# Banded attention: one sequence of projection pieces for all pairs, kept two pieces ahead of the tiles

## The chip, the cores and the metric

The kernel runs on one core of a Trainium2 chip. Its engines are TensorE (PE: matmuls, with their weight loads, PEld), VectorE (DVE), ScalarE (ACT), GpSimd (POOL) and SyncE (SP, which issues most DMAs). Each takes its instructions in order and waits for the others by semaphores. The metric is the time of one execution on the device in microseconds, less is better. Three runs of the kernel before took 1625.54 to 1629.71 us, 1628.01 in the median.

## The reference

One layer of a bidirectional encoder over 1024 tokens of width 1024, in float32. The part that the change touches, shortened:

```python
h = rms_norm(x)
q_lat, kv_lat, q_b, k_b, v_b, gate_a, gate_b = split(h @ w_in)
o_a = mla_branch(q_lat, kv_lat, ...)      # dense attention, 8 heads
# windowed branch: 16 heads of 64, 4 key/value heads, |i-j| <= 128
s = q @ k.T * scale + bias;  s = where(valid, s, -1e30)
p = softmax(concat([s, sink]))[..., :span]
o_b = p @ v
mixed = sigmoid(gate_a) * o_a + sigmoid(gate_b) * o_b
x = x + mixed @ w_out                     # then a convolutional FFN
```

## The kernel before

Float32 operands are split into a rounded high part and the rest (`split`: a cast on ScalarE, L132, and a subtraction on VectorE, L133), and a product is three matmuls on these parts. The kernel goes through norm and latents, the banded (windowed) branch with the projections of gates, queries and keys, the dense branch, and the FFN. The change is in the banded branch, from about 138 to 534 us of the span.

The banded branch goes over 8 pairs of heads (`t`, 0 to 7) and in each over 8 tiles of 128 rows (`n`, 0 to 7). A tile has three stages on TensorE. `s1` makes the scores of the next tile (L138, `sc`) and hands them to VectorE (L657: bias, mask and minimum), ScalarE (L661: two exponentials with their sums) and GpSimd (L666: normalisation). `s2` turns the tile's probabilities with five transposes into the one PSUM buffer `ptw` (L679) and splits them in three parts, one wide (128x512) and two narrow (64x128), into `pth` (L132) and `ptl` (L133). `s3` multiplies the previous tile's parts with the values (`po`); ScalarE copies half of that (L702), VectorE adds (L704), and half a pair at a time VectorE multiplies by a gate (L709).

Between the stages stand pieces of the projections `h @ w_in` for the gates of this pair and the queries of the next: a generator `project` makes one 128x512 block in 24 matmuls (L446), and it yields after every six, a piece. With a block's last piece comes its end: a copy on VectorE for a gate (L507) and later a sigmoid on ScalarE (L511), a cast (L493) and a subtraction (L494) per half for queries, and twice two of each for keys (L474 to L477). Weights come by DMA (L106), are cast on ScalarE (L110, `whi`) and subtracted on GpSimd (L113, `wlo`); the queue of buffers lets them run ahead. Exponential and sigmoid need different tables on ScalarE, so each sigmoid among the exponentials brings two table loads.

A pair has 24 pieces and 24 stages, and behind each stage one piece follows (L764 to L766). Pair 3 makes the keys for pairs 4 to 7 in place of two gate blocks; pair 7 makes those two, spreads 22 of its 24 pieces over the stages and hands the rest to the end, where buffers of the normed input are refilled for the dense branch.

The order on TensorE is the program's up to tile 5 of pair 7 (`manual_schedule`); on the other engines, and on TensorE after that, a scheduler orders the instructions as it thinks they become ready.

Of the kernel before, what the change touches and what calls it, by code (L numbers as in the profile page):

```python
# [23 lines left out]
NT = S // P  # L24
KD = D // P
# [20 lines left out]
C_GA = C_V + KV_B * HD_B  # L46
C_GB = C_GA + D
# [13 lines left out]
FIRST = "PE Activation".split()  # L61
ORDER = 'b0 a0 A0 d0 b1 a1 A1 d1'.split()
PRE = 2
END = 22
DEFER = 3
ABS = 2
# [8 lines left out]
def f32(ap):  # L75
    return ap.bitcast(F32)
# [3 lines left out]
def encoder_layer(ctx, tc, x, positions, norm1_g, w_in, q_a_norm_g, w_q_b, kv_a_norm_g, w_kv_b,  # L80
# [101 lines left out]
    def big(shape, name):  # L182
        return hp.tile(shape, F32R, tag="big", bufs=4, name=name)
# [233 lines left out]
    def absorbing(u):  # L417
        h = u % H_A
        return weights4(wqk_d.rearrange("k p h c -> p k h c")[:, :, h:h + 4, :], 2, 4, P)
# [4 lines left out]
    def absorb_into(u, pair, pj):  # L424
        qs[u] = pair
        h, hf = u % H_A, u // H_A
        tok = slice(hf * 512, (hf + 1) * 512)
        terms = []
        for k in range(2):
            wh, wlo = [w[:, k, h % 4] for w in wqk[u // 4]]  # L430
            terms += [(wh, lt["h"][:, k, tok]), (wh, lt["l"][:, k, tok]), (wlo, lt["h"][:, k, tok])]
        three(pj, terms)
        split(pair[0], pair[1], pj)


    with ExitStack() as pa:
# [3 lines left out]
        def project(w, hf, post):  # L440
            hi, lo = w()
            pj = ps.tile([P, 512], F32, tag="pj", bufs=3, name="pj")
            tok = slice(hf * 512, (hf + 1) * 512)
            for k in range(KD):
                for j, (a, b) in enumerate(((hi, ht_h[hf]), (hi, ht_l[hf]), (lo, ht_h[hf]))):
                    nc.tensor.matmul(pj, a[:, k, :], b[:, k], start=(k + j == 0), stop=(k == KD - 1 and j == 2))  # L446
                if k % 2 == 1:
                    if k == KD - 1:
                        post(pj, tok)
                    yield  # L450

        def once(c0):
            got = []

            def w():
                if not got:
                    got.append(columns(w_in, c0, P))
                return got[0]
            return w
# [3 lines left out]
        def keys(g):  # L463
            w = once(C_K + g * HD_B)

            def post(pj, tok):
                if tok.start == 0:
                    for gg in (g, g + 1):
                        kws[gg] = [ap_.tile([P, S], F32R, tag="kw", bufs=6, name="kw") for _ in range(2)]
                for j in range(2):  # L470
                    kh, kl = kws[g + j]
                    a = slice(j * HD_B, (j + 1) * HD_B)
                    b = slice((1 - j) * HD_B, (2 - j) * HD_B)
                    nc.scalar.copy(kh[a, tok], pj[a, :])  # L474
                    nc.scalar.copy(kh[b, tok], pj[a, :])
                    nc.vector.tensor_tensor(kl[a, tok], pj[a, :], f32(kh[a, tok]), op=ALU.subtract)
                    nc.vector.tensor_tensor(kl[b, tok], pj[a, :], f32(kh[a, tok]), op=ALU.subtract)  # L477
            return [project(w, hf, post) for hf in range(2)]
# [3 lines left out]
        def queries(t):  # L482
            w = once(C_Q + t * P)

            def post(pj, tok):
                hf = tok.start // 512
                qss[t, hf] = ap_.tile([P, 512 // HQ, 2, HQ], F32R, tag="qs", bufs=4, name="qs")
                for j in range(2):
                    q_ = qss[t, hf][:, :, j]
                    a = slice(j * HD_B, (j + 1) * HD_B)  # L490
                    b = slice((1 - j) * HD_B, (2 - j) * HD_B)
                    src = pj[a, :].rearrange("p (m c) -> p m c", c=HQ)
                    nc.scalar.mul(q_[a], src, HD_B ** -0.5)  # L493
                    nc.vector.scalar_tensor_tensor(q_[b], src, HD_B ** -0.5, f32(q_[a]),  # L494
                                                   op0=ALU.mult, op1=ALU.subtract)
            return [project(w, hf, post) for hf in range(2)]
# [3 lines left out]
        def gates(t, name, c0):  # L500
            w = once(c0 + t * P)

            def post(pj, tok):
                hf = tok.start // 512
                g_ = ap_.tile([P, 512], F32, tag="g", bufs=6, name="g")
                gts[t, name, hf] = g_
                nc.vector.tensor_copy(g_, pj)  # L507
                apart = t == DEFER
                if (name, hf) == ("a", 1) or (apart and hf == 1):
                    for nm_, h_ in ((name, 0), (name, 1)) if apart else (("b", 0), ("b", 1), ("a", 0), ("a", 1)):  # L510
                        nc.scalar.activation(gts[t, nm_, h_], gts[t, nm_, h_], AF.Sigmoid)  # L511
                    for h_ in range(2 if name == "a" else 0):
                        nc.sync.dma_start(ga_d[t][:, h_ * 512:(h_ + 1) * 512], gts.pop((t, "a", h_)))
            return [project(w, hf, post) for hf in range(2)]
# [89 lines left out]
        def dense_start(j):  # L604
            if j == 1:
                for j in range(2):
                    lt[j] = big([P, H_A, 512], f"qr{j}")
                    for c in range(0, H_A, 2):
                        nc.sync.dma_start(f32(lt[j][:, c:c + 2]), qr_d[j][:, c:c + 2])
                return  # L610
            for nm_, d_ in (("h", lt_d[0]), ("l", lt_d[1])):
                lt[nm_] = big([P, 4, S], "lt_" + nm_)
                for c in range(4):
                    nc.sync.dma_start(f32(lt[nm_][:, c]), d_[:, c])
            return
            yield

        def absorb_early(u):
            raw = wp.tile([P, 2, 512], F32R, tag="raw", bufs=2, name="qearly")
            absorb_into(u, [raw[:, j] for j in range(2)], ps.tile([P, 512], F32, tag="pj", bufs=3, name="pje"))  # L620
            return
            yield
# [89 lines left out]
        def drain(gen):  # L712
            for _ in gen:
                pass
# [16 lines left out]
        drain(q0_[0])  # L731
        s1(0, 0)
        drain(q0_[1])
        def steps():
            for t in range(KD):
                gb, ga = gates(t, "b", C_GB), gates(t, "a", C_GA)
                if t < KD - 1:
                    q_ = queries(t + 1)
                    gens = [gb[0], gb[1], ga[0], q_[0], ga[1], q_[1]]
                    if t == DEFER:  # L740
                        gens = [gb[0], gb[1], q_[0], q_[1]]
                    total = 24
                    if t % 4 == 3:
                        gens += keys((t + 1) // 2)
                        total = 24
                else:
                    gens = [dict(b=gb, a=ga, A=gates(DEFER, "a", C_GA), d=[dense_start(0), dense_start(1)])[c][int(i)] for c, i in ORDER] + [absorb_early(u) for u in range(PRE)]
                    total = END
                chain_ = (None for gen in gens for _ in gen)
                done, pos = 0, 0  # L750
                for n in range(NT):
                    for stage in range(3):
                        if stage == 0:
                            if n + 1 < NT:
                                s1(t, n + 1)
                            elif t + 1 < KD:
                                s1(t + 1, 0)
                        elif stage == 1:
                            s2(t, n)
                        elif n > 0:  # L760
                            s3(t, n - 1)
                        elif t > 0:
                            s3(t - 1, NT - 1)
                        pos += 1  # L764
                        while done < math.ceil(total * pos / 24):
                            next(chain_, None)  # L766
                            done += 1
                    if n == NT - 1:
                        drain(chain_)
                    if (t, n) == (KD - 1, ABS):  # L770
                        wqk[0] = absorbing(0)
                    yield t, n

        todo = steps()
        with tc.manual_schedule(engines={mybir.EngineType.PE}):
            while next(todo) != (KD - 1, MANUAL):
# [54 lines left out]
    with ExitStack() as pb:  # L831
# [143 lines left out]
        for i in range(ni):  # L975
            u, qt = i // 4, i % 4
# [30 lines left out]
        u = ni // 4 - 1  # L1007
# [151 lines left out]
    gens = [preps(f) for f in range(NF)]  # L1159
# [205 lines left out]
    with ExitStack() as pe_:  # L1365
# [40 lines left out]
        for gi, group in enumerate(groups):  # L1406
# [3 lines left out]
            for bank, phase, outs in phases:  # L1410
# [9 lines left out]
                for j, tp in turns_:  # L1420
                    if up_ and j == 0:
                        banks[bank, tp] = ps.tile([P, 512], F32, tag=bank, bufs=4, name="b" + bank)
                    a, w = opers[j]
# [5 lines left out]
                for tp in range(4):  # L1429
                    b_ = banks[bank, tp]  # L1430
                    i = outs[0] * 4 + tp
# [49 lines left out]
```

## Time and profile before

| | |
|---|---|
| runs | 1625.54, 1628.01, 1629.71 us |
| profiled execution | 1627.23 us, span 1625.5 us |
| busy, share of the span | PE 1583.6 us (97%), DVE 1121.9 (69%), ACT 902.8 (56%), POOL 539.8 (33%) |
| largest groups of the banded branch | projections (L446) x416 of each of three forms, 169.2, 164.4 and 164.0 us |

The times of a group are sums over its instructions. Matmuls are pipelined: one of 128x512 is shown with 0.39 to 0.40 us, and the next starts 0.23 us after it. An idle time in brackets is that of the engine just before the row's instruction, with what ended it. Engines wait for each other, so a busy share says little by itself; the waits of TensorE say where time can be won. The page's clock line shows TensorE at full clock in every slice.

### The profile page before, as it was taken

The numbers are of one execution on the slowest core, as the hardware profiler recorded it, in microseconds if no ns is written. First come the engines' busy times: TensorE is split into PE (matmuls) and PEld (weight loads), VectorE is DVE, ScalarE is ACT, GpSimd is POOL, SyncE is SP. The second block draws the span as 40 slices with busy tenths as digits, with TensorE's granted clock in tenths as the row PEclk, the third lists the DMA queues.
The fourth block names the chain that finished last, engine by engine and source line by source line (L and its number), as shares of the span: only waits on it lengthen the run. The fifth ranks groups of instructions, "written<-read, shape, count | busy, mean of one in ns | idle before, by whom it ended". The sixth has DMA issues, their size and how long they took to land.

```text
span 1625.5 us, 21901 instructions
## 1 busy us (share of the span) xinstructions
PE 1583.6 (97%) x7714; PEld 1306.1 (80%) x7714; DVE 1121.9 (69%) x2024; ACT 902.8 (56%) x1688; POOL 539.8 (33%) x487
## 2 busy tenths in 40 slices
PE   8999999999999899999999999999999999999998
PEld 7887888878888778888887777888888888778886
DVE  6575655666655576666663388777777777799997
ACT  6446777777777565555552255445444444443445
POOL 3113343434342475656562000344443343000011
PEclk9999999999999999999999999999999999999999
DMA  8472211111213551113124883222222221652402
GB/s 272 123 208 73 66 51 58 52 56 51 69 47 131 192 196 61 62 50 129 52 78 156 291 297 91 78 79 79 90 79 78 78 91 65 262 193 77 156 1 104
DMA packets 151893, 179.57 MB, mean 110 GB/s; under 512 B 10711, under 2 KB 112903, under 8 KB 151784
## 3 DMA queue, kind: packets, MB, share of 16 engines
q1 hardware_dynamic: 149160, 169.59, 31.8%
q0 software_dynamic: 2624, 8.59, 1.6%
q8 instruction: 61, 1.00, 0.3%
q14 instruction: 48, 0.39, 0.1%
HBM read 126.74 MB, written 51.41 MB: 110 GB/s over the span
## 4 chain that ended last, share of the span: by engine, by line
PE 68%; ACT 4%; DVE 4%; DMA 3%; issue 1%; SPq 0%; POOL 0%; ACTq 0%; DVEq 0%
PE bx L1155 15%; PE byz L1155 11%; PE sc L138 9%; PE bx L1427 6%; PE po L138 6%; PE by L1427 6%; PE pj L446 5%; PE pt L876 3%; PE py L138 2%; DMA mh<-mx_d 1%; PE pjq L138 1%; PE pyb L138 1%; PE ptw L679 1%; DMA x_d<-xt 1%; PE pjo L138 1%
## 5 line engine op out<-in xcount | busy, mean ns | idle before, releaser
L1155 PE MATMUL bx<-hs,op 128*128 128x512 f32 x1056 | 258.6, 395 | 0.9 <-ACT hs L1203 0.7
L1155 PEld LDWEIGHTS bx<-hs,op 128*128 128x128 f32 x1056 | 198.0, 188 | 49.6 <-ACT hs L1203 0.9
L1155 PE MATMUL byz<-hs,op 128*128 128x512 f32 x792 | 196.3, 395 | 0.0
L1155 PEld LDWEIGHTS byz<-hs,op 128*128 128x128 f32 x792 | 148.6, 188 | 36.4 <-DVE hs L788 0.4
L446 PE MATMUL pj<-ht_h,whi 128*128 128x512 f32 x416 | 169.2, 407 | 0.0
L446 PE MATMUL pj<-ht_h,wlo 128*128 128x512 f32 x416 | 164.4, 395 | 0.0
L446 PE MATMUL pj<-ht_l,whi 128*128 128x512 f32 x416 | 164.0, 394 | 0.0
L862 POOL TENSOR_TENSOR p<-p,rib 128x1024 f32<-128x1024 f32 x64 | 123.4, 1938 | 119.2 <-DVE rib L861 99.0
L788 POOL TENSOR_TENSOR op<-wu,op 128x512 fp32r<-128x512 f32 x38 | 48.9, 1298 | 273.4 <-DVE cg L791 149.4
L132 ACT CAST pT<-pt 128x512 fp32r<-128x512 f32 x128 | 73.5, 589 | 92.0 <-PE pt L876 91.9
L133 DVE TENSOR_TENSOR ptl<-ptw,pth 64x128 fp32r<-64x128 f32 (+2 forms) x176 | 74.4, 423 | 72.0 <-ACT pth L132 69.9
L788 POOL TENSOR_TENSOR op<-s,op 128x512 fp32r<-128x512 f32 x57 | 99.0, 1736 | 66.0 <-ACT op L1026 65.8
L133 DVE TENSOR_TENSOR pT<-pt,pT 128x512 fp32r<-128x512 f32 x128 | 86.8, 682 | 46.2 <-ACT pT L132 46.1
L1427 PE MATMUL bx<-op,op 128*128 128x512 f32 x480 | 113.6, 394 | 3.3 <-ACT cv L1350 1.8
L1427 PEld LDWEIGHTS bx<-op,op 128*128 128x128 f32 x480 | 90.9, 190 | 23.7 <-ACT cv L1350 2.2
L113 POOL TENSOR_TENSOR wlo<-raw,whi 128x512 fp32r<-128x512 f32 x66 | 85.4, 1321 | 65.6 <-ACT whi L110 65.2
L1427 PE MATMUL by<-op,op 128*128 128x512 f32 x444 | 103.6, 389 | 0.0
L854 DVE TENSOR_REDUCE nmb<-sc 128x1 f32<-128x1024 f32 x64 | 78.3, 1224 | 35.4 <-PE sc L138 34.9
L666 POOL TENSOR_TENSOR st<-st,ri 128x640 f32<-128x640 f32 x48 | 60.1, 1251 | 115.7 <-DVE ri L663 115.5
L1427 PEld LDWEIGHTS by<-op,op 128*128 128x128 f32 x444 | 83.1, 188 | 17.9 <-DVE x L791 0.4
L138 PE MATMUL po<-pT,ct 128*128 128x512 f32 x384 | 94.6, 395 | 0.0
L138 PE MATMUL sc<-lt_h,q 128*128 128x512 f32 x224 | 93.5, 417 | 1.2 <-ACT p L859 1.2
(297 smaller groups left out, 3651.2 us busy)
## 6 DMA issues: line engine op xcount, KB each, us to landing
wu<-in_w_up_dram SPq DMA_DIRECT2D x44, 512.0 KB, 3.8
raw<-in_w_in_dram SPq DMA_DIRECT2D x29, 512.0 KB, 3.9
act_d<-t SPq DMA_DIRECT2D x22, 512.0 KB, 2.6
ra<-act_d SPq DMA_DIRECT2D x22, 512.0 KB, 5.1
rw<-in_w_down_dram SPq DMA_DIRECT2D x22, 512.0 KB, 4.9
mh<-mx_d SPq DMA_DIRECT2D x16, 512.0 KB, 5.2
mh<-mx_d SPq DMA_DIRECT2D x12, 448.0 KB, 3.5
xt<-in_x_dram SPq DMA_DIRECT2D x8, 512.0 KB
```

What stands on the lines that cost most here:

```text
L113: nc.gpsimd.tensor_tensor(lo[:, q], raw[:, q], f32(hi[:, q]), op=ALU.subtract)
L132: nc.scalar.copy(hi, src)
L133: nc.vector.tensor_tensor(lo, src, f32(hi), op=ALU.subtract)
L138: nc.tensor.matmul(ps, a, b, start=(i == 0), stop=(i == n - 1))
L446: nc.tensor.matmul(pj, a[:, k, :], b[:, k], start=(k + j == 0), stop=(k == KD - 1 and j == 2))
L666: nc.gpsimd.tensor_tensor(pn, pn, ri[:, :, None].broadcast_to([P, 2, BAND]), op=ALU.mult)
L788: eng.tensor_tensor(dst, a, b, op=ALU.subtract)
L854: nc.vector.tensor_reduce(nm, sc, axis=AX.X, op=ALU.max, negate=True)
L862: nc.gpsimd.tensor_tensor(pe, pe, ri.broadcast_to([P, S]), op=ALU.mult)
L876: nc.tensor.transpose(pt[:, c, :], pe[:, kcol:kcol + P], ident)
L1155: nc.tensor.matmul(bank, a[:, i, k], hs[c][:, j, k], start=(start and k + n == 0), stop=(k == 3 and n == 2), skip_group_check=not start)
L1427: nc.tensor.matmul(banks[bank, tp], l_, r_, start=(up_ and j + n == 0), stop=(j == len(group) - 1 and n == 2), skip_group_check=not up_)
```

## The change

The pieces of all pairs form one sequence, made by the new function `pieces`, and each stage takes pieces up to its own place plus `LEAD_A`, which is 2. So three pieces stand behind the first stage, one behind each further stage, and the last pair ends its pieces two stages earlier. Before, each pair had its own sequence, which ended with the pair's last stage. What is computed is the same.

```diff
+LEAD_A = 2
...
@@ -731,23 +732,20 @@
         drain(q0_[0])
         s1(0, 0)
         drain(q0_[1])
+        def pieces(t):
+            gb, ga = gates(t, "b", C_GB), gates(t, "a", C_GA)
+            if t == KD - 1:
+                made = dict(b=gb, a=ga, A=gates(DEFER, "a", C_GA), d=[dense_start(0), dense_start(1)])
+                return [made[c][int(i)] for c, i in ORDER] + [absorb_early(u) for u in range(PRE)]
+            q_ = queries(t + 1)
+            if t == DEFER:
+                return [gb[0], gb[1], q_[0], q_[1]] + keys((t + 1) // 2)
+            return [gb[0], gb[1], ga[0], q_[0], ga[1], q_[1]]
+
         def steps():
+            chain_ = (None for t in range(KD) for gen in pieces(t) for _ in gen)
+            done = 0
             for t in range(KD):
-                gb, ga = gates(t, "b", C_GB), gates(t, "a", C_GA)
-                if t < KD - 1:
-                    q_ = queries(t + 1)
-                    gens = [gb[0], gb[1], ga[0], q_[0], ga[1], q_[1]]
-                    if t == DEFER:
-                        gens = [gb[0], gb[1], q_[0], q_[1]]
-                    total = 24
-                    if t % 4 == 3:
-                        gens += keys((t + 1) // 2)
-                        total = 24
-                else:
-                    gens = [dict(b=gb, a=ga, A=gates(DEFER, "a", C_GA), d=[dense_start(0), dense_start(1)])[c][int(i)] for c, i in ORDER] + [absorb_early(u) for u in range(PRE)]
-                    total = END
-                chain_ = (None for gen in gens for _ in gen)
-                done, pos = 0, 0
                 for n in range(NT):
                     for stage in range(3):
                         if stage == 0:
@@ -761,11 +759,12 @@
                             s3(t, n - 1)
                         elif t > 0:
                             s3(t - 1, NT - 1)
-                        pos += 1
-                        while done < math.ceil(total * pos / 24):
+                        pos = 3 * n + stage + 1
+                        due = (KD - 1) * 24 + math.ceil(END * pos / 24) if t == KD - 1 else t * 24 + pos
+                        while done < due + LEAD_A:
                             next(chain_, None)
                             done += 1
-                    if n == NT - 1:
+                    if (t, n) == (KD - 1, NT - 1):
                         drain(chain_)
                     if (t, n) == (KD - 1, ABS):
                         wqk[0] = absorbing(0)
```

The scheduled engines are ordered anew. The line numbers of the changed kernel are one higher there. On ScalarE, tile 1 of pair 1 before: from the wide cast of that tile's chain to that of the next. `pth` are the casts of the split, `kr` is the copy, `st` the exponentials, `g` the sigmoid, `whi` the cast of projection weights.

```order
L132 CAST pth<-ptw 128x512
L511 ACT_TABLE_LOAD
L511 ACTIVATE g<-g 128x512
L132 CAST pth<-ptw 64x128
L702 COPY kr<-po 64x256
L132 CAST pth<-ptw 64x128
L661 ACT_TABLE_LOAD
L661 ACTIVATE st,sm<-st,nm 128x321 x2
L132 CAST pth<-ptw 128x512
```

The same tile after the change:

```order
L133 CAST pth<-ptw 128x512
L133 CAST pth<-ptw 64x128
L703 COPY kr<-po 64x256
L133 CAST pth<-ptw 64x128
L111 CAST whi<-raw 128x1024
L512 ACT_TABLE_LOAD
L512 ACTIVATE g<-g 128x512
L662 ACT_TABLE_LOAD
L662 ACTIVATE st,sm<-st,nm 128x321 x2
L133 CAST pth<-ptw 128x512
```

The sigmoid with its load stood inside the tile's chain of casts; now it stands behind it, with a weight cast ahead of it.

On VectorE, tile 4 of pair 3, before: from the wide subtraction of its chain to the reciprocal of a later softmax. `ptl` are the chain's subtractions, `nm` with `st` the passes over the scores, the first `ob` the adds, the second the product with the gate, `qs` the queries' subtraction.

```order
L133 TENSOR_TENSOR ptl<-ptw,pth 128x512
L133 TENSOR_TENSOR ptl<-ptw,pth 64x128
L704 TENSOR_TENSOR ob<-po,kr 64x128 x2
L133 TENSOR_TENSOR ptl<-ptw,pth 64x128
L709 TENSOR_TENSOR ob<-ob,g 128x512
L657 ISA st,nm<-sc,bt,nsink 128x320
L657 ISA nm 128x1
L657 ISA st,nm<-sc,bt,nsink 128x320
L657 ISA nm 128x1
L663 RECIPROCAL ri<-sm 128x2
```

The same tile after the change:

```order
L134 TENSOR_TENSOR ptl<-ptw,pth 128x512
L495 SCALAR_TENSOR_TENSOR qs<-pj,qs 64x8x64
L134 TENSOR_TENSOR ptl<-ptw,pth 64x128
L705 TENSOR_TENSOR ob<-po,kr 64x128 x2
L658 ISA st,nm<-sc,bt,nsink 128x320
L658 ISA nm 128x1
L658 ISA st,nm<-sc,bt,nsink 128x320
L658 ISA nm 128x1
L710 TENSOR_TENSOR ob<-ob,g 128x512
L495 SCALAR_TENSOR_TENSOR qs<-pj,qs 64x8x64
L134 TENSOR_TENSOR ptl<-ptw,pth 64x128
L664 RECIPROCAL ri<-sm 128x2
```

Before, the chain's last subtraction came ahead of the gate product and the scores; now scores, gate product and a subtraction of the queries stand ahead of it.

## Rows read from the trace of the kernel before

**Rows 1.** Waits of TensorE, 120 to 525 us: total us, times, longest.
```profile
PE ptw L679 <- DVE ptl L133: 7.7, 17, 1.5
PE ptw L679 <- POOL st L670: 1.8, 2, 1.6
```

**Rows 2.** Timeline of TensorE: the turns; start, us each, idle before.
```profile
186.01 0.63 PE L679 MATMUL ptw<-ident,st 128*128 128x128 f32 x4 [0.25 <-DVE ptl L133]
...
191.94 0.60 PE L679 MATMUL ptw<-ident,st 128*128 128x128 f32 x4
...
197.60 0.71 PE L679 MATMUL ptw<-ident,st 128*128 128x128 f32 x5
...
203.40 0.71 PE L679 MATMUL ptw<-ident,st 128*128 128x128 f32 x5
...
209.61 0.74 PE L679 MATMUL ptw<-ident,st 128*128 128x128 f32 x5
...
215.65 0.71 PE L679 MATMUL ptw<-ident,st 128*128 128x128 f32 x5
...
221.65 0.71 PE L679 MATMUL ptw<-ident,st 128*128 128x128 f32 x5
...
228.10 0.74 PE L679 MATMUL ptw<-ident,st 128*128 128x128 f32 x5 [0.38 <-DVE ptl L133]
...
234.43 0.63 PE L679 MATMUL ptw<-ident,st 128*128 128x128 f32 x4 [0.21 <-DVE ptl L133]
```

**Rows 3.** Timeline of ScalarE, tiles 3 to 6 of pair 1.
```profile
215.37 0.63 ACT L511 ACTIVATE g<-g 128x512 f32<-128x512 f32 x1
...
216.02 1.28 ACT L661 ACT_TABLE_LOAD   x1
...
217.32 0.57 ACT L661 ACTIVATE st<-st,nm 128x321 f32<-128x321 f32 x1
...
218.55 0.59 ACT L132 CAST pth<-ptw 128x512 fp32r<-128x512 f32 x1
...
220.57 0.26 ACT L132 CAST pth<-ptw 64x128 fp32r<-64x128 f32 x1
...
224.06 0.59 ACT L493 ACTIVATE qs<-pj 64x512 fp32r<-64x512 f32 x1
...
230.12 1.05 ACT L110 CAST whi<-raw 128x1024 fp32r<-128x1024 f32 x1
```

**Rows 4.** Timeline of VectorE, tiles 4 and 5 of pair 1.
```profile
221.19 0.29 DVE L133 TENSOR_TENSOR ptl<-ptw,pth 64x128 fp32r<-64x128 f32 x1
...
221.51 0.69 DVE L709 TENSOR_TENSOR ob<-ob,g 128x512 f32<-128x512 f32 x1
...
222.24 0.55 DVE L657 CUSTOM_DVE_ANT_0 st<-sc,bt,nsink 128x320 f32<-128x320 f32 x1
...
224.69 0.68 DVE L494 SCALAR_TENSOR_TENSOR qs<-pj,qs 64x512 fp32r<-64x512 f32 x1 [0.45 <-ACT qs L493]
...
227.66 0.29 DVE L133 TENSOR_TENSOR ptl<-ptw,pth 64x128 fp32r<-64x128 f32 x1
```

**Rows 5.** The chain of waits: one piece of six projection matmuls.
```profile
334.26 1.39 PE pj L446 x6
```

**Rows 6.** Timeline of TensorE: the first turn.
```profile
142.76 0.33 PE L679 MATMUL ptw<-ident,st 128*128 128x128 f32 x1 [1.61 <-POOL st L670]
```

**Rows 7.** Timeline of TensorE: two turns of pair 3.
```profile
325.30 0.74 PE L679 MATMUL ptw<-ident,st 128*128 128x128 f32 x5 [0.69 <-DVE ptl L133]
...
333.63 0.63 PE L679 MATMUL ptw<-ident,st 128*128 128x128 f32 x4 [1.51 <-DVE ptl L133]
```

**Rows 8.** Timeline of ScalarE: the latents land at the dense branch's start.
```profile
546.72 1.31 ACT L132 CAST ct<-craw 128x512 fp32r<-128x512 f32 x2 [3.91 <-DMA craw<-lat_d]
```

**Rows 9.** Timeline of TensorE: the wait behind it.
```profile
551.43 0.80 PE L138 MATMUL sc<-lt_h,qearly 128*128 128x512 f32 x1 [4.34 <-ACT p L859]
```

**Rows 10.** Windows: PE, PEld, DVE, ACT, POOL busy, granted clock, DMA share, GB/s.
```profile
551.40:555.00 3.60, 3.57 (x9) 2.85 (x10) 1.52 (x4) 3.08 (x5) 1.95 (x2) 0.54 0.47 136
```

## The prediction

> **What bounds the kernel now.** The page's first part (the table above) comes first: TensorE is busy nearly all the time, so only its idle gaps can be won, and only work put in its way can lose. Then the waits of TensorE in the banded stretch: nearly all of them are at the turns (`ptw`, the transposes of a tile's probabilities), 17 of them for the last small subtraction `ptl` on VectorE, 7.7 us, and two at the start for the normalised probabilities, 1.8 us [rows 1]. Nothing else there is worth a microsecond. So the question is one: when is the single `ptw` bank free again?
>
> The turns of one pair in order of time show the pace [rows 2]. From turn to turn tile 0 takes 5.66 us, tile 1 5.80, tile 2 6.21, tile 3 6.04, tile 4 6.00, tile 5 6.45 and tile 6 6.33; the last two hold listed waits of 0.38 and 0.21. Tile 7, seen at the pair's start, takes 5.93.
>
> What frees the bank is a chain on two in-order engines: wide cast on ScalarE, wide subtraction on VectorE, narrow cast, narrow subtraction, copy and adds of the previous tile, narrow cast, narrow subtraction. Undisturbed it takes from the wide cast at 218.55 [rows 3] to the end of the subtraction at 221.19 + 0.29 = 221.48 [rows 4]: 2.93 us, and ScalarE is free at 220.57 + 0.26, which is 2.3 us after the cast began. A turn follows 0.15 us behind the last subtraction (227.66 + 0.29, turn at 228.10) [rows 2, 4]. So a tile that is bound by the chain lasts its *lag* + 2.93 + 0.15, where the lag is how long after its turn the wide cast starts. At tile 4 of this pair it was 218.55 - 215.65 = 2.90, which ends at 5.83 and just fits.
>
> The lag is made by what stands before the cast on ScalarE. A tile's score pass on VectorE starts at 222.24, and its two exponentials are done at 224.06, 1.82 later [rows 3, 4]. Where a sigmoid came between, the return load (1.28), the two exponentials and the gap to the cast take 218.55 - 216.02 = 2.53; load and sigmoid before them 1.29 + 0.65 = 1.94; a weight cast takes 1.05, a query cast 0.60 [rows 3].
>
> **The change, part by part.** No matmul, pass, load or byte is added or removed. Two pieces of six matmuls, 1.39 us each [rows 5], move ahead of the first turn, and from there every piece stands two stages earlier against the tiles. The ends of the projections, with their casts, copies and sigmoids, so fall into other tiles, and ScalarE, VectorE, GpSimd and SP are ordered anew around them.
>
> *Start.* Before, the first turn waits for GpSimd [rows 6]. Two more pieces, 2.8 us, now stand ahead of it. That covers the listed 1.8 and the drained pipe around it: at least 1.8, at most 2.8; I take -2.3. Nothing is late next, since TensorE then reaches the turn about when the normalisation ends.
>
> *An ordinary pair* (1, 2, 5 and 6). I lay the changed order of ScalarE and VectorE out with the durations above, each tile's times counted from its turn.
> Tile 7 ends bound by its chain, so tile 0 begins with a lag of 1.82 - 0.15 = 1.67. Its short chain leaves ScalarE at 3.4; then load and sigmoid, return load and exponentials, 1.94 + 2.53, end at 7.9. Less the tile's 5.66 that is a lag of 2.2 for tile 1. There the casts end at 4.5, and behind them now stand weight cast, load, sigmoid, return load and exponentials: 4.5 + 1.05 + 1.94 + 2.53 = 10.0, less 5.80 a lag of 4.2 for tile 2. Before, the sigmoid stood inside tile 1's own chain, which had room, and the weight cast a tile later. Tile 2 so lasts 4.2 + 3.08 = 7.3 against 6.21: +1.1.
> Tile 3 fits. In tile 4 both query subtractions (0.68 each) and the gate product (0.69) now stand inside the chain [rows 4]: lag 1.6, and from 2.2 on VectorE has 0.7 + 0.7 + 0.3 + 0.6 + 0.7 + 0.7 + 0.3, so the next turn comes at 6.4 against 6.00: +0.4. Tile 5 loses the wait it had: -0.5. But behind its casts stand again a weight cast (it waits for the matmuls of a gate's last piece, done at some 4.1: the turn and the weighted sum, 1.2, and two pieces), two loads and a sigmoid: 4.1 + 1.05 + 1.94 + 2.5 - 6.0 = 3.6 of lag for tile 6, which lasts 6.65 against 6.33: +0.3. In tile 7 weight cast and query cast stand ahead of the wide cast, and the turn comes at 6.25 against 5.93: +0.3. Sum per pair +1.6, four times: +6.4.
>
> *Pair 0* starts with a lag of only 1.2 in tile 1, so that its tile 2 is no worse than before; its other tiles as above: +0.2. *Pair 4* begins early: tile 2 only +0.3, the rest +0.5, together +0.8.
>
> *Pair 3* has the key projections. Before, they cost the turns at 325.30 and 333.63 waits of 0.69 and 1.51, and the tile between these two turns lasts 8.33 us [rows 7]. Now the keys end two stages earlier, and the tiles need only 5.9: -0.8 and -2.4. But tile 2 pays its +1.1 as in other pairs; in tile 4 VectorE has the score pass of the tile after next, the gate product and a query subtraction ahead of the chain's last subtraction: those scores are there at 4.6, and 1.0 + 0.7 + 0.7 + 0.3 later, with adds not yet done by then and the turn's 0.15, it is 7.6 to 8.0 against 6.0: +2.0; and in tile 7 two key subtractions stand at that place, as in the 8.33 us tile: +2.4. Together +2.3.
>
> *Pair 7.* Tile 3 now has a table load and a sigmoid inside its chain, 1.94, where it had one weight cast of 1.05: +1.0, and tile 2 +0.1.
>
> *Behind the banded part.* The last projection stands at the same place among TensorE's matmuls as before. It frees the buffers for the rotated queries, and the latents that are loaded behind these land at 546.72 [rows 8]; TensorE waits 4.34 us for what hangs on them [rows 9]. All of this moves along with the last projection. That the last tile now has its turn later (some 1.5 us of new wait) is covered by these 4.34 us; without that cover it would be +1.5.
>
> Sum: -2.3 + 6.4 + 0.2 + 0.8 + 2.3 + 1.1 = +8.5 us. No lag of 4.2 is in the trace of before; the nearest row is the 2.90 above, and if lags stayed there, ordinary pairs would cost nothing and only the start and the keys would count, about -2: the low end. At the high end each weight cast waits a further microsecond for its matmuls, one lag more in six pairs: +14. I take +8.5, for laid out in the same way the old order gives a lag of 2.8 for tile 4 of the pair shown, and the rows have 2.90.
>
> A load in this trace takes 1.28 us, and the exponential behind it starts 0.02 later (216.02, 217.32) [rows 3]. The Trainium skill (ScalarE: Activation LUTs, "What ACT_TABLE_LOAD costs") adds a drain of about 1.38 us to each switch, 2.66 in all. By that, tile 2's lag would be 2.8 longer, and the change would cost some 10 us more; the trace shows no such drain behind a load.
>
> **Rivals.** *The other side:* the gaps go and nothing comes. The sigmoids leave most chains, ScalarE has idle time between these, and if the cast of tile 2 begins with a lag under 2.96 (6.04 - 3.08), no turn there waits. For it: the start's and the keys' waits are real. It gives -2.3, the keys' -3.2 and up to -0.6 in each of six other pairs: 1619 to 1623, say 1622. Against it: the order of ScalarE puts 1.05 + 1.94 + 2.53 = 5.5 us of work behind tile 1's last cast.
> *No net change:* the lags come out a microsecond shorter (weight casts that fall into idle time), and start and keys pay for the rest: 1628 to 1632, say 1630.
> *Half clock:* behind the wait of 4.34 us the granted clock is 0.54, the lower of the two levels, over 3.6 us [rows 10], which costs 1.7. The page's clock line shows no fall behind the waits of 1.61 and 1.51. If it falls behind the three waits near 2 us that I expect in pairs 3 and 7, that is 3 x 1.7 = +5: 1642. The Trainium skill (TensorE: Matmul & The Clock Gate, "Part 1") has the engine go back to half clock when it has idled.
>
> **How the numbers follow.** The profiled execution took 1627.23, its span 1625.5; the sum is made there, and the median of the runs, 1628.01, is 0.8 above it. I add the sum to the median: 1636.5. Chances: forecast 0.62 (its own range 1632.5 to 1640), half clock 0.06, no net change 0.2, the other side 0.12. A change under 0.3% (4.9 us) can't be told from none here. Slower by more: nearly all of the first two and a tenth of the third, 0.70; within: 0.19; faster by more: 0.11. The range reaches into the third case, 1628.5, and above to 1642.
>
> **What would show it.** In the new trace: no wait for GpSimd at the first turn; waits for `ptl` of about 1.1 us at the turns into tile 3 of pairs 1, 2, 5 and 6, and smaller ones into tiles 5, 7 and 0; in pair 3 two waits of about 2 us, into its tile 5 and into pair 4; the wait of 4.34 us at the start of dense attention still there or a little shorter. Wrong it is if the turn into tile 3 comes on time: then the lag did not build up, and the time is 1630 or less.

## The result and the profile after

The changed kernel takes 1635.22 us (median of 6 runs, 1633.21 to 1636.88 and one of 1640.85) against 1626.62 for the kernel before on the same chip: a ratio of 1.0051, 95% interval 1.0041 to 1.0062. That is 8.6 us slower. The profiled execution took 1635.3, its span 1633.5, 8.0 above the span before. Line numbers of the changed kernel differ by one from those before (the turn is now line 680, the pieces 447, the sigmoid 512); in kernels of the experiments that add lines they differ by more.

The waits of TensorE in the same stretch, 120 to 525 us, answer to [rows 1] (columns as there):

```profile
PE ptw L680 <- DVE ptl L134: 16.2, 18, 2.4
PE sc L139 <- DVE nm L658: 0.3, 1, 0.3
```

The waits for GpSimd are gone, and the wait for the chain's last subtraction has doubled. The first two turns, against [rows 6]; the first now comes without a wait:

```profile
143.77 0.60 PE L680 MATMUL ptw<-ident,st 128*128 128x128 f32 x4
148.97 0.71 PE L680 MATMUL ptw<-ident,st 128*128 128x128 f32 x5
```

The turns of pair 1 from its tile 0 to tile 5, against [rows 2]:

```profile
192.41 0.63 PE L680 MATMUL ptw<-ident,st 128*128 128x128 f32 x4
198.12 0.71 PE L680 MATMUL ptw<-ident,st 128*128 128x128 f32 x5
203.93 0.71 PE L680 MATMUL ptw<-ident,st 128*128 128x128 f32 x5
211.29 0.74 PE L680 MATMUL ptw<-ident,st 128*128 128x128 f32 x5 [1.19 <-DVE ptl L134]
217.36 0.71 PE L680 MATMUL ptw<-ident,st 128*128 128x128 f32 x5
223.66 0.74 PE L680 MATMUL ptw<-ident,st 128*128 128x128 f32 x5
```

Tile 2 lasts 211.29 - 203.93 = 7.36 us, before 6.21. The cause stands on ScalarE, in its timeline from tile 1 to tile 2 of that pair:

```profile
202.38 0.26 ACT L133 CAST pth<-ptw 64x128 fp32r<-64x128 f32 x1
202.67 1.05 ACT L111 CAST whi<-raw 128x1024 fp32r<-128x1024 f32 x1
203.74 1.28 ACT L512 ACT_TABLE_LOAD   x1
205.03 0.64 ACT L512 ACTIVATE g<-g 128x512 f32<-128x512 f32 x1
205.69 1.28 ACT L662 ACT_TABLE_LOAD   x1
206.98 0.57 ACT L662 ACTIVATE st<-st,nm 128x321 f32<-128x321 f32 x1
...
207.54 0.55 ACT L662 ACTIVATE st<-st,nm 128x321 f32<-128x321 f32 x1
...
208.21 0.59 ACT L133 CAST pth<-ptw 128x512 fp32r<-128x512 f32 x1
```

Read it from the top: the last cast of tile 1 ends at 202.64, and weight cast, load, sigmoid, return load and both exponentials follow with no gap above 0.03 us. The wide cast of tile 2 starts 208.21 - 203.93 = 4.28 us after its turn, and the next turn comes 211.29 - 208.21 = 3.08 us behind that cast. The turns of pair 3 and of pair 7 that wait longest:

```profile
324.93 0.74 PE L680 MATMUL ptw<-ident,st 128*128 128x128 f32 x5 [1.67 <-DVE ptl L134]
...
345.23 0.63 PE L680 MATMUL ptw<-ident,st 128*128 128x128 f32 x4 [2.43 <-DVE ptl L134]
...
520.19 0.83 PE L680 MATMUL ptw<-ident,st 128*128 128x128 f32 x5 [1.91 <-DVE ptl L134]
```

Behind the last two the clock falls, as windows show (columns as in [rows 10]; the sixth figure behind the length, 0.52 and 0.50, is the granted clock, close to the lower of the two levels, 1.2 GHz):

```profile
346.50:350.00 3.50, 3.50 (x12) 2.92 (x11) 2.33 (x6) 1.62 (x3) 0.24 (x2) 0.52 0.02 5
521.00:524.00 3.00, 3.00 (x10) 2.44 (x9) 1.14 (x3) 0.88 (x3) 1.46 (x3) 0.50 1.03 380
```

At the start of dense attention, the wait that answers to [rows 9], and a new one in the last banded tile:

```profile
545.96 0.36 PE L139 MATMUL po<-pth,vw 128*128 128x256 f32 x1 [1.30 <-DVE ob L705]
...
561.84 0.79 PE L139 MATMUL sc<-lt_h,qearly 128*128 128x512 f32 x1 [2.82 <-ACT p L858]
```

The old wait shrank from 4.34 to 2.82, which covers the new one of 1.30. Dense attention so starts 561.84 - 551.43 = 10.4 us later than before, and the kernel ends 8.0 later.

### The profile page after: what moved, and what is told of

Its sections match the earlier page's. It is cut to its first block, busy times and chain, and to the rows that moved or that the text cites. A ratio compares the mean times of both kernels' runs of the same rounds, so it can differ in the third digit from the quotient of the medians.

```text
span 1633.5 us, 21920 instructions
## 1 busy us (share of the span) xinstructions
PE 1584.9 (97%) x7714; PEld 1310.2 (80%) x7714; DVE 1123.0 (69%) x2024; ACT 903.8 (55%) x1687; POOL 538.2 (33%) x485
## 4 chain that ended last, share of the span: by engine, by line
PE 80%; ACT 8%; DVE 6%; issue 4%; DMA 1%; POOL 0%; SPq 0%; ACTq 0%; DVEq 0%; POOLq 0%
PE bx L1154 15%; PE byz L1154 11%; PE pj L447 10%; PE sc L139 9%; PE po L139 7%; PE bx L1426 6%; PE by L1426 6%; PE py L139 4%; PE pt L875 3%; ACT st L662 2%; PE ptw L680 1%; DVE ptl L134 1%; PE pv L139 1%; ACT pth L133 1%; PE pjq L139 1%
```

## The experiments

The theory: start and key waits are really gone, but in the new phase of the pieces weight cast, load and sigmoid stand together behind a tile's last cast; ScalarE so reads the one `ptw` bank late, and the next turn waits for it. Rivals: running ahead or joining the sequences costs as such; VectorE or the matmuls themselves make the waits; the bank is not what the turn waits for. By "the one bank" the text means the one buffer `ptw`, of 8 x 128 columns, twice the 512 of a `pj` buffer: four blocks for the wide transposes and one for the narrow. Each ratio is to the kernel before, with its 95% interval.

**The lead in pair 0 alone.**

```diff
-                        while done < due + LEAD_A:
+                        while done < due + (LEAD_A if t == 0 else 0):
```

> The lead of two pieces holds in pair 0 alone; in the first two stages of pair 1 no projection piece is issued, and from there the sequence stands as before the change. Theory (the start is really won, and the lag of ScalarE behind the new phase costs 1.4 to 1.5 us in each of the pairs 1, 2, 5 and 6, and more in 3 and 4): the start's -2.3 stays and the rest of the loss goes, 1623 to 1625; waits for ptl at the turns into tile 3 of pairs 1 to 6 again under 0.3. Rival (joining the sequences or the new first stage is what costs): 1632 or more. Rival (the start is a shift that is given back later): 1626 to 1628.

Measured 1627.28, ratio 1.0004 (0.9995 to 1.0014): no change. The waits into tile 3 of pairs 1 to 3 are gone, as the theory has it, and tile 2 of pair 1 lasts 6.21 again; so joining the sequences is not what costs. But the start's gain wasn't kept: the time lies outside the 1623 to 1625 of the theory and in the range of the rival by which the start is given back. The turns around the stretch without pieces:

```profile
185.82 0.63 PE L680 MATMUL ptw<-ident,st 128*128 128x128 f32 x4 [0.54 <-DVE ptl L134]
191.96 0.63 PE L680 MATMUL ptw<-ident,st 128*128 128x128 f32 x4 [1.45 <-DVE ptl L134]
196.27 0.71 PE L680 MATMUL ptw<-ident,st 128*128 128x128 f32 x5
```

Where a piece is missing, TensorE stands before the turn for 1.45 us, because the chain does not get shorter with the matmuls. At the turn of tile 1 of pair 0 the kernel is 2.7 ahead of before (148.53 less the two pieces' 2.78, against 148.48), at 196.27 only 1.3 (197.60), at the start of dense attention 1.5 (549.97 against 551.43), and at the end of the span 0.3; why the rest is lost behind dense attention was not tried. A lead is borrowed matmul work: where it is given back, a chain may show that the work hid.

**A lead of three pieces,** a whole tile.

```diff
-LEAD_A = 2
+LEAD_A = 3
```

> A lead of three pieces, which is one whole tile, in place of two. Theory (the phase of the pieces against the tiles decides, not the lead): the ends of the pieces fall at the same stage of a tile as before the change, so load, sigmoid and weight cast stand inside chains again and not together behind a last cast; start -2 to -3, pairs within 0.5 of before each, 1622 to 1628. Rival (running ahead as such costs, by the buffers or the casts that come early): 1635 or more, and more than with two pieces.

Measured 1635.45, ratio 1.0041 (1.0028 to 1.0055). Pair 1 lasts 242.99 - 194.29 = 48.70 us, before 48.46, with a lead of two 49.89; pairs 2, 4, 5 and 6 lose 0.3 to 0.4 each. So phase, not lead, makes the ordinary pairs slow. Yet the time is as bad, where the theory had 1622 to 1628: in pair 3 2.0 us are lost, and from the start of pair 7 to dense attention 6.4, with a turn in tile 4 behind which the clock is 0.58 for 4 us (that tile lasts 10.89), and a wait of 1.96 for a cast:

```profile
515.44 0.73 PE L680 MATMUL ptw<-ident,st 128*128 128x128 f32 x5 [2.02 <-DVE ptl L134]
...
539.33 0.38 PE L139 MATMUL po<-pth,vw 128*128 128x256 f32 x1 [1.96 <-ACT pth L133]
```

The number of the rival (running ahead as such costs) was met. Since the ordinary pairs lose so little, running ahead alone does not cost much; what makes pairs 3 and 7 lose with a lead of three was not tried.

**Two banks, first try,** in the new and the old order.

```diff
-            pt = ps.tile([P, 8, P], F32, tag="pt", bufs=1, name="ptw")
+            pt = ps.tile([P, 4, P], F32, tag="pt", bufs=2, name="ptw")
+            pn = pon[:, 2 + n % 2]
...
-            po = ps.tile([P, 512], F32, tag="po", bufs=1, name="po")
+            po = pon.rearrange("p c q -> p (c q)")
```

> The changed kernel with a second ptw bank: the narrow transpose goes to the unused half of the po bank, so that the wide transposes of successive tiles use two banks in turn. Theory (the turn waits only because the one bank is still being read by the late casts): the 16.2 us of waits for ptl go, and with them the half clock behind two of them (3.3 us): 1614 to 1621. The scores' exponentials are done 4 us after a turn at the worst, and the normalisation takes 1.5, so a wait for GpSimd of up to 0.5 may show in a few tiles. Rival (the turns wait for the late work of ScalarE in any case, by the exponentials): the waits move to st, and the time stays above 1630.

> The kernel before with the same second ptw bank. Theory: its 7.7 us of waits for ptl go, the start's 1.8 us for GpSimd stay: 1617 to 1621. Against the changed kernel with two banks it is then slower by the start, 1 to 3 us, where with one bank it was faster by 8.6. Rival (the change costs by something else than the bank): it stays some 8 us faster than the changed kernel with two banks.

Measured 1775.11 (1.0910, 1.0895 to 1.0925) and 1732.27 (1.0644, 1.0627 to 1.0662). No turn waits for `ptl` any more, but the weighted sums do. The waits of the new order, 120 to 545 us:

```profile
PE pon L139 <- DVE ptl L134: 85.8, 41, 3.6
```

The tile shared by `po` and the narrow transposes joins two chains that had been apart. Whether the program's dependences or the bank itself ask for that wait, these runs don't tell; for the question they tell nothing.

**No table loads,** in both orders.

```diff
-                        nc.scalar.activation(gts[t, nm_, h_], gts[t, nm_, h_], AF.Sigmoid)
+                        nc.scalar.activation(gts[t, nm_, h_], gts[t, nm_, h_], AF.Exp)
```

> The changed kernel with Exp in place of Sigmoid at the gates (the gates' values are so not the reference's): the order of every engine stays, and only the table loads around the sigmoids go. Theory (the lag of ScalarE makes the new waits; in the tile before the wait of 1.2 us it holds two loads of 1.28): the waits at the turns into tile 3 of pairs 1, 2, 3, 5 and 6 go entirely, those into tile 7 too; what VectorE alone makes stays, 0.5 into tile 0, 1.7 and 2.4 in pair 3. About 1.2 + 0.2 us in each of five pairs and 2 to 4 us in pair 7 and its half clock: 1625 to 1629. Rival (the waits come from VectorE's order or from the matmuls themselves): they stay, and the time stays above 1633.

> The kernel before with the same Exp for Sigmoid, as the control. Theory: its waits were made by VectorE (0.4 and 0.2 in a pair, the keys' 0.7 and 1.5), so only the wait of pair 7 (1.1) and the first ones go: 1624 to 1627. The changed kernel without loads is then within 4 us of it, where with loads it is 8.6 slower. Rival: the loads cost both orders the same, 5 us or more each, and 8 us stay between the two.

Measured 1619.10 (0.9955, 0.9943 to 0.9968) and 1618.13 (0.9944, 0.9932 to 0.9956). Of the 8.6 us between the orders 1.0 is left. Apart from the loads, the order of ScalarE's instructions is that of the changed kernel in its whole stretch from 140 to 525 us. The new order's waits for `ptl` to 525 us:

```profile
PE ptw L680 <- DVE ptl L134: 4.7, 3, 2.4
```

The other fifteen are gone, and the three that stay are those at which VectorE is late (1.67 and 2.41 in pair 3, 0.58 in pair 7). Tile 2 of pair 1 lasts 6.01. Both kernels came out 6 us below the range expected. The loads had more to give than the theory had it: the small waits of 0.2 to 0.4 in each pair of the old order had been put down to VectorE, and they went with the loads too, as did those of 0.5 in the new order.

**Two banks, second try:** the narrow transpose has its own bank and stands behind the next piece; the bank comes from `pj`.

```diff
-            pj = ps.tile([P, 512], F32, tag="pj", bufs=3, name="pj")
+            pj = ps.tile([P, 512], F32, tag="pj", bufs=2, name="pj")
...
-            pt = ps.tile([P, 8, P], F32, tag="pt", bufs=1, name="ptw")
+            pt = ps.tile([P, 4, P], F32, tag="pt", bufs=2, name="ptw")
...
+        def s2n(n):
+            pth, ptl = pths[n % 2]
+            pn = ps.tile([P, P], F32, tag="pn", bufs=1, name="ptn")
+            nc.tensor.transpose(pn, mid[0][:, 1 + 2 * P:1 + 3 * P], ident)
...
-                        elif n > 0:
-                            s3(t, n - 1)
+                        else:
+                            s2n(n)
+                            if n > 0:
+                                s3(t, n - 1)
```

> The changed kernel with two banks for the wide transposes and a bank of its own for the narrow one, which moves behind the next projection piece (the banks come from the third buffer of pj). The earlier pair put the narrow one into the po bank, and po waited for it. Theory (the one bank, read late, is what the turns wait for): the 16.2 us of waits for ptl fall under 4 us, the half clock behind two of them goes too, and the time is 1615 to 1624 unless the third pj buffer is missed (a wait of pj for the copies of a piece's end, up to 1 us for each of 60 pieces: up to 1675). Rival (the work of ScalarE is late in any case): the waits move to st or pth, and nothing is won.

> The same three banks in the kernel before. Theory: its 7.7 us of waits go, 1617 to 1623 by the same condition, and the two orders differ by the start alone, 1 to 3 us in favour of the new one. Rival: the new order stays 5 us or more slower with two banks as well.

Measured 1615.15 (0.9930, 0.9917 to 0.9944) and 1620.22 (0.9957, 0.9945 to 0.9970). No turn waits for `ptl` in either. The longest wait of the new order to 525 us is the price of the missing third buffer:

```profile
PE pj L447 <- DVE kw L478: 1.3, 1, 1.3
```

With the bank free in time the change turns round: the new order is 5.1 us faster, where with one bank it is 8.6 slower. The expectation had 1 to 3 for the start alone. The spans of the two profiles are 5.9 apart, and 1.7 of that arise in the first half of the FFN, which runs at two paces that nothing here ties to the change (last section); in the old order tile 0 of pair 0 also lasts 7.25 us (5.72 in the kernel before), with a granted clock of 0.59 from 146.5 to 149.5.

**One bank each for the wide and the narrow transposes,** the third `pj` buffer kept: as above, with

```diff
-            pt = ps.tile([P, 8, P], F32, tag="pt", bufs=1, name="ptw")
+            pt = ps.tile([P, 4, P], F32, tag="pt", bufs=1, name="ptw")
```

> The changed kernel with the third pj buffer kept and one bank each for the wide and the narrow transposes, the narrow one behind the next projection piece. Of the two-bank kernel it lacks the second wide bank. Theory (what holds the turn is the end of the chain, so it is enough that the wide bank is read out first): the wide bank is free at the lag + 1.3, at the latest 5.5 us after its turn, before the next; waits for ptl under 3 us in all; the 2.5 us that the first turn lost with two pj buffers come back: 1611 to 1616. Rival (two wide banks are needed, or the moved narrow transpose meets its own late chain): 1620 or more.

> The same split in the kernel before. Theory: without waits for the bank the two orders differ by the start, 2 to 4 us in favour of the new one: 1614 to 1619. Rival: no difference, or the old order ahead.

Measured 1611.07 (0.9897, 0.9884 to 0.9911) and 1616.63 (0.9937, 0.9924 to 0.9951). The first beats both kernels, by 17 us (the kernel before took 1628.05 beside it) and some 24, in the same number of banks. In pair 1 its turns and last subtractions stand so (TensorE, then VectorE):

```profile
201.25 0.60 PE L680 MATMUL ptw<-ident,st 128*128 128x128 f32 x4
203.10 0.27 PE L690 MATMUL ptn<-ident,st 128*128 128x128 f32 x1
207.29 0.60 PE L680 MATMUL ptw<-ident,st 128*128 128x128 f32 x4
```

```profile
205.39 0.69 DVE L134 TENSOR_TENSOR ptl<-ptw,pth 128x512 fp32r<-128x512 f32 x1 [0.44 <-ACT pth L133]
...
206.80 0.30 DVE L134 TENSOR_TENSOR ptl<-ptn,pth 64x128 fp32r<-64x128 f32 x1
```

The wide bank is read out at 206.08, 1.2 us before its next turn, although ScalarE is still late (wide cast at 204.77, 3.5 behind the turn). A second wide bank is not needed. But ScalarE's order was made anew here too: the lag of this tile is 3.5 in place of 4.28, and its whole chain ends at 207.10, also before the next turn. Tile 4 of pair 3 separates the two. Its last subtraction (on VectorE) comes as late as in the changed kernel, whose next turn waited for it until 324.93:

```profile
324.49 0.29 DVE L134 TENSOR_TENSOR ptl<-ptw,pth 64x128 fp32r<-64x128 f32 x1
```

With the split bank (TensorE, then VectorE):

```profile
307.81 0.60 PE L680 MATMUL ptw<-ident,st 128*128 128x128 f32 x4
313.82 0.60 PE L680 MATMUL ptw<-ident,st 128*128 128x128 f32 x4
```

```profile
315.18 0.29 DVE L134 TENSOR_TENSOR ptl<-ptn,pth 64x128 fp32r<-64x128 f32 x1
```

The chain ends 7.66 us after the tile's turn, before the split 7.70, and yet the next turn comes after 6.01, ahead of the chain's end. Eight turns of this profile do so; with one buffer, in the kernel before and in the changed one, none of 63 does. So it is the buffer that a turn waits for.

The difference of 5.6 between the orders is more than the 2 to 4 expected. In the old order the start has its old wait, and here the clock fell behind it:

```profile
142.63 0.33 PE L679 MATMUL ptw<-ident,st 128*128 128x128 f32 x1 [1.61 <-POOL st L670]
143.20 0.44 PE L679 MATMUL ptw<-ident,st 128*128 128x128 f32 x2 [0.24 <-POOL st L670]
```

```profile
144.00:147.00 3.00, 3.00 (x10) 2.27 (x9) 0.84 (x2) 0.41 (x2) 1.40 (x2) 0.53 0.26 79
```

Its tile 0 lasts 7.29 us, 5.72 in the kernel before: 1.6 for the clock, 2.9 for the start, and 0.6 in tile 6 of pair 3 make 5.1 of the 5.6.

**Idle matmuls in the two long waits** of the changed kernel.

```diff
+                            if (t, n) in {(4, 0): 9, (7, 4): 7}:
+                                fill = ps.tile([P, 512], F32, tag="pj", bufs=3, name="fill")
+                                for _ in range({(4, 0): 9, (7, 4): 7}[t, n]):
+                                    nc.tensor.matmul(fill, ht_h[0][:, 0, :P], ht_h[0][:, 0], start=True, stop=True)
                             s2(t, n)
```

> The changed kernel with idle matmuls (nobody reads what they write) in the two waits behind which the clock fell to half: nine ahead of the turn into pair 4 (2.05 us of a wait of 2.43) and seven ahead of the turn of tile 4 of pair 7 (1.6 us of 1.91). Theory (the fall follows the idle stretch, and each costs about 1.6 us): the granted clock stays at 1.00, tile 0 of pair 4 lasts 5.7 instead of 7.24 and tile 4 of pair 7 8.1 instead of 9.73, 1631 to 1633. Rival (the fall has another cause, or the tiles are long by their own waits): both tiles last as before and the time stays 1635.

**The changed kernel once more.**

> The changed kernel once more, for what repeats in its profile. Theory: the turns' waits (1.2 into tile 3, 2.4 into pair 4, 1.9 in pair 7) and the two falls of the clock are the same to 0.1 us, and the banded stretch ends 10 us later than before. The 1.6 us that the FFN's first half was faster than before are a matter of the run, since the old order without loads had them too and the start-only kernel not: they may be missing here.

The two belong together. With the fill 1634.22 (1.0044, 1.0031 to 1.0056), between the 1631 to 1633 of the theory and the 1635 of the rival and not told apart from 1635.22; the second run, one execution, gave 1633.91. The turns around the start of pair 4, with the fill, and the window behind:

```profile
342.71 2.20 PE L760 MATMUL fill<-ht_h 128*128 128x512 f32 x9
345.27 0.63 PE L680 MATMUL ptw<-ident,st 128*128 128x128 f32 x4 [0.37 <-DVE ptl L134]
350.98 0.71 PE L680 MATMUL ptw<-ident,st 128*128 128x128 f32 x5
```

```profile
346.00:349.00 3.00, 3.00 (x16) 2.52 (x15) 2.12 (x6) 1.85 (x4) 0.79 (x2) 1.00 0.02 5
```

The turn comes when it came without the fill, but the clock stays up and the tile lasts 5.71 instead of 7.24. In the second run of the unfilled kernel it fell there again (tile of 7.16), but not in pair 7:

```profile
520.01 0.74 PE L680 MATMUL ptw<-ident,st 128*128 128x128 f32 x5 [1.92 <-DVE ptl L134]
528.16 0.71 PE L680 MATMUL ptw<-ident,st 128*128 128x128 f32 x5
```

That tile takes 8.15 without any fill, 8.15 with it, and in the first profile 9.73 behind the same wait. For pair 4 the clock fell in both profiles without the fill and held in the one with it, which speaks for the fill; since the falls differ between runs, one profile does not prove it. For pair 7 no effect is shown. That "the two falls are the same" was wrong; the waits themselves repeated within 0.1.

## Why the prediction was right, and where not

The time was right (1636.5 against 1635.22) and so was the mechanism. Most terms came out as worked. That the total is this close is in part luck: two errors of opposite sign cancelled, some 2.7 us too little in pairs 4 and 7 and 2.4 given back behind the banded part. The table is made from the turns of the two profiles, with the 2.78 us of two pieces taken off where they stand earlier. Of the kernel before it needs, beside [rows 2] and [rows 9], the turn of tile 1 of pair 0 and those that begin pairs 3 and 4; of the changed one, the turn that begins pair 3 (pair 5 begins at 388.12 before and at 395.83 after, pair 7 at 484.92 and 495.56):

```profile
148.48 0.71 PE L679 MATMUL ptw<-ident,st 128*128 128x128 f32 x5
...
288.80 0.60 PE L679 MATMUL ptw<-ident,st 128*128 128x128 f32 x4
...
339.58 0.60 PE L679 MATMUL ptw<-ident,st 128*128 128x128 f32 x4
```

```profile
292.17 0.63 PE L680 MATMUL ptw<-ident,st 128*128 128x128 f32 x4
```

| Step | predicted | measured |
|---|---|---|
| start, to the turn of tile 1 | -2.3 | 148.97 - 148.48 - 2.78 = -2.3 |
| rest of pair 0 | +0.2 | 0.0 |
| pairs 1, 2, 5, 6 | 4 x 1.6 = +6.4 | 1.43 + 1.47 + 1.48 + 1.45 = +5.8 |
| pair 3 | +2.3 | 53.06 - 50.78 = +2.3 |
| pair 4 | +0.8 | 50.60 - 48.54 = +2.1 |
| pair 7 to dense start | +1.1 | 10.4 - 7.9 = +2.5 |
| behind it | 0 | 8.0 - 10.4 = -2.4 |

*The lag.* It was to be 2.2 in tile 1 and 4.2 in tile 2, with 3.08 to the next turn. The rows have 200.37 - 198.12 = 2.25, then 4.28 and 3.08. No such lag stood in the trace of before; the order of ScalarE and the durations of its instructions gave it. That loads are what fills it, the kernels without loads show, and that the single bank turns it into a wait, those with the split bank: each takes the waits away without touching the order of the pieces. Tile by tile pair 1 changed by +1.15 in tile 2, +0.3 in tile 4, -0.5 in tile 5, +0.3 in tile 6 and +0.2 in tile 7, where +1.1, +0.4, -0.5, +0.3 and +0.3 were worked out. Of the smaller waits that were to be seen, into tiles 5, 7 and 0, only the one into tile 7 is listed (0.50).

*Pair 3.* Both waits of about 2 us came (1.67 into tile 5, 2.43 into pair 4), and the keys' old ones [rows 7] are gone. Tiles 2, 4, 5, 6 and 7 changed by +1.1, +1.8, -0.8, -2.5 and +2.5, where +1.1, +2.0, -0.8, -2.4 and +2.4 were worked out. These two waits are VectorE's: they stay without the loads.

*Half clock.* This was a rival with a chance of 0.06, left out of the sum. It came true in part: behind two of the three waits in the first profile, one of three in the second. Pair 4's excess of 1.3 over the forecast is this term (its tile 0 lasts 7.24 instead of 5.68): with the fill, where the clock held, pair 4 is 0.84 longer than before, as forecast. So is pair 7's: in the second run, where the clock held there, dense attention starts 8.7 us late (560.10) instead of 10.4, and pair 7's part of that is 1.0, forecast 1.1. I had taken it as rare because the waits of 1.61 and 1.51 in [rows 6, 7] had no fall behind them. For that the prediction names the page's clock line, which can't show it: a 9 there means 90% or more, and the slice with the fall of [rows 10] has its 9 too. Windows of the kernel before behind the two waits do show it:

```profile
142.70:146.00 3.30, 3.00 (x14) 2.41 (x15) 1.70 (x4) 1.79 (x5) 1.96 (x4) 1.00 0.60 157
333.70:337.00 3.30, 3.30 (x20) 2.91 (x21) 1.04 (x3) 1.11 (x3) 1.20 (x3) 1.00 0.00 0
```

New waits longer than any in the banded branch before deserved more. The Trainium skill (TensorE: Matmul & The Clock Gate, "Part 1") has idling send the engine back to half clock. The rows agree in that the falls follow idle stretches; they do not show a fall behind each.

*Behind the banded part.* The step that did not hold is "all of this moves along with the last projection". It holds through dense attention (10.2 us late at its end, 898.03 against 887.85). Then 1.0 is given back in the output projection (the waits for `mh` shrink there from 1.1 to 0.5) and 1.8 in the FFN's first half, and 0.6 is lost again in its second. Whether the 1.8 are the change's is open (last section). The 1.0 came in both profiles of the changed kernel (1.0 and 1.1), but the other kernels differ there from the kernel before by -0.5 to +1.3, whichever their order; its cause was not tried.

*The rivals.* The other side failed at the point named for it: the lag of tile 2 was 4.28, not under 2.96. The rival of no net change asked for lags a microsecond shorter. As to the load: here too the exponential starts 0.01 us behind the return load (205.69 + 1.28, 206.98), so the drain that the Trainium skill states (ScalarE: Activation LUTs, "What ACT_TABLE_LOAD costs") is again not in the rows, and 10 us more did not come. The prediction's low end of about -2 would be 1626, while the range that it states begins at 1628.5; the result touches neither.

## What to carry to other kernels

When a sequence is moved against a pipeline of tiles, lay out the in-order engine that reads the shared bank, with the durations of the old profile: what stands between a tile's last cast and the next tile's first says which turn will wait, before any run. Before tuning such a phase, look whether the bank has to be held that long: giving the wide and the narrow part a bank each, with the narrow transpose a piece later, made the same reordering worth 5.6 us (1.6 of them a fall of the clock in the old order) instead of costing 8.6. And work that is run ahead hides a chain's latency only while it stands there; where it is given back, the wait returns.

## What was not expected of the hardware

The clock's fall is not told by the length of the wait before it. It fell behind 2.43 and 2.41 us in both profiles of the changed kernel, but not behind 2.41 at the same place in the kernel without loads; behind 1.91 in one profile and not behind 1.92 in the other; behind 1.61 and 0.24 in the old order with the split bank, and not behind the same two waits in the kernel before.

Within the FFN's first half, from 1100 to 1300 us, TensorE never waits and the granted clock is 1.00, and still there are two paces. These 200 us of the changed kernel, then of the kernel before (each row from its own profile):

```profile
1100.00:1300.00 200.00, 200.00 (x863) 162.13 (x862) 151.31 (x143) 96.74 (x145) 80.68 (x52) 1.00 0.25 82
```

```profile
1100.00:1300.00 200.00, 200.00 (x858) 160.85 (x857) 150.88 (x143) 95.20 (x142) 79.48 (x52) 1.00 0.25 79
```

The records hold 863 matmuls against 858; from the first `bx` matmul of that half to the first of the second half it took 434.5 us against 436.3. Of the kernels in the old order, the one without loads (863) and the one with the split bank (862) ran at the faster pace, and the one with two banks (859) at the slower, as did the one with the lead in pair 0 alone (859). All those with a lead throughout ran at the faster. So the old order does not force the slower pace; what sets it stays open, and a difference of 1.8 us between two profiles may come from here and not from an edit.
